# Hybrid encoder layer on one core: the warm-up's tile, the squares of x, the order of SyncE's transfers and the return of the gated heads

## The chip, the cores and the metric

The kernel runs on one core of one Trainium2 chip. The metric is device time in microseconds; the program is run several times and the median counts. All matrix work is in 32-bit floats, split in two parts as told below.

## The reference, cut to what matters

One layer of the encoder is computed: pre-norm, neighbourhood attention over an 8 x 64 grid of tokens, a gate, the projection out, post-norm, residual. With 512 tokens, width 2048, 16 heads of 128:

```
h = x * rsqrt(mean(x*x) + eps) * g_pre
q, k, v, z = split(h @ w_in)            # 2048 x 8192
o = softmax(q k^T * scale + bias) v     # keys: all 8 rows, 16 columns round the query's
y = (o * silu(z)) @ w_out               # 2048 x 2048
out = x + y * rsqrt(mean(y*y) + eps) * g_post
```

## The kernel before, in words

**Split operands.** Each matrix operand is split into `hi` (a cast on ScalarE, ACT, L227) and `lo` (the rest, a subtraction on VectorE, DVE, L228), and a product is three matmuls: hi by hi, hi by lo, lo by hi. The part of x is called `a` (L136, L137), after a scaling by the pre-norm's gain (L140, `gcol`).

**Blocks.** The main loop (L662) walks over blocks m. A block is one k tile of 128 rows: a weight tile of 128 x 512 is brought in (`raw`, four buffers, or `T`, eight tiles), split (three buffers of `hi` and of `lo`), and multiplied with the parts of x. `prep` (L217) of a block runs two blocks ahead of its matmuls, and at its end issues later loads (`load_raw`, `load_t`).

- Blocks 0 to 31 (`mm_first`, L264) are the projection in for heads 0 and 1, twelve matmuls each. In the first sixteen x comes in too (`load_x`, L129, three blocks ahead of its own).
- Then seven steps, one for each further pair of heads, of seven passes of eight blocks with six matmuls each (`mm_in`, L285; accumulators u1X to u7Z by step and chain). This is a product in seven instead of eight parts, so weights are added up on VectorE first (`t<-t,raw`, L224). The fifth and the seventh pass of a step load new T tiles while raws come in.
- Blocks 424 to 487 (`mm_out`, L629) are the projection out, four quarters n of sixteen blocks, twelve matmuls each.

**Beside the blocks.** `at(m, f)` hangs work on a block: for each head the transposes (`turn`, L358), the splits of q and k, the scores (L422, tiles `s`), the bias table (`load_bias`, `bias`, L405: `braw` and `bm`), exponentials and normalization (`edge`, `p`), the second transpose and its split (`pt`), the product with v (L492, `o`), the gate (`gate0` to `gate2`, `gated`, `zm`). While step s is projected, the heads of the pair before are attended to; heads 14 and 15 run in the projection out. The gated heads 0 to 13 are written to memory by GpSimd (`graw`, L504), come back late in step 7 and in the projection out (`gr`, L514, one tile of the tag "z" each), and are split into `g` (L520, L521) for the blocks of the projection out: head k in block k of each quarter.

**Squares.** Sixteen tiles of x in token order (`square_x`, `sq`) are squared and summed on ScalarE (L164) for the pre-norm; `rstd` turns the sums into `rc`, with which the results of the projection are scaled (`take_first`, L271).

**What sets the order.** Each engine runs its instructions in one queue, and SyncE (SP) issues nearly all loads in one queue too: a load that waits for its buffer holds the loads behind it. The code is written in the order of the blocks, but a scheduler sorts each engine's queue when the program is built, by its own estimate of when things are ready. So the written order and the built order differ. Pools matter: the tag "c" has six pair tiles (128 x 2 x 512) that hold the results of a pair's projection, and later `yg`.

**The warm-up.** Eight small matmuls of the identity (`warm`, L86, sixteen records in the trace) are written first, to keep TensorE busy until there is data.

Of the kernel before, what the change touches and what calls it, by code (L numbers as in the profile page):

```python
# [15 lines left out]
P = 128  # L16
# [34 lines left out]

@with_exitstack
def na_block(ctx: ExitStack, tc: tile.TileContext, xT, x, gpre, gpost, w_in, w_out, rpb, mask, out):
    nc = tc.nc
    PSUM = bass.MemoryType.PSUM
# [27 lines left out]
    make_identity(nc, ident)  # L83
    warm = px.tile([P, P], F32, tag="T", name="warm")
    for i in range(WARM):
        nc.tensor.matmul(warm, ident, ident, start=True, stop=True)  # L86
# [26 lines left out]
    def load_t(step, q, k):  # L113
        nc.sync.dma_start(T[k], w_in[step, q, k])
# [4 lines left out]
    def load_x(k):  # L119
        kk = k % KH  # L120
        if k >= KH:
            X[k] = small("v" if kk < 4 else "z", f"x{k}")
        elif kk < 4:
            X[k] = small("qk", f"x{k}")
        else:
            if kk % 2 == 0:
                X["c", kk] = pair(f"x{k}")
            X[k] = X["c", kk - kk % 2][:, kk % 2, :]
        nc.sync.dma_start(X[k], xT[k])  # L129
# [25 lines left out]
    def square_x(i):  # L155
        j, n = divmod(i, 4)
        ns = slice(n * L, (n + 1) * L)
        t = sp.tile([P, L], F32, tag=("bm", "braw")[i % 2], name=f"sq{i}")
        if j == 0:
            nc.sync.dma_start(t[0:64, :], x_v[56:64, :, ns])  # L160
            nc.sync.dma_start(t[64:128, :], x_v[0:8, :, ns])
        else:
            nc.sync.dma_start(t, x_v[16 * j - 8 : 16 * j + 8, :, ns])
        return lambda: nc.scalar.activation(t, t, AF.Square, accum_out=part[:, j, n : n + 1])  # L164
# [31 lines left out]
    def load_raw(m):  # L196
# [10 lines left out]
        nc.sync.dma_start(raws[m], src)  # L207
# [299 lines left out]

    def split_g(h):

        if h in g_of:  # L510
            g = g_of[h]
        else:
            g = small("z", f"gr{h}")
            nc.gpsimd.dma_start(g, graw[h])  # L514

        def go():
            k, o = h % KH, h // KH
            t = ag.tile([P, 2, L], F32R, tag=f"a{k}_{1 - o}", name=f"g{h}")
            hi, lo = t[:, 0, :], t[:, 1, :]
            nc.scalar.copy(hi, g)  # L520
            nc.vector.tensor_tensor(lo, g, hi.bitcast(F32), ALU.subtract)  # L521
            G[h] = (hi, lo)

        return go
# [32 lines left out]
    def when(h, c):  # L557

        pr, b = divmod(h, 2)
        m = base(pr + 1)  # L560
        return m + c + (3, 26)[b] if pr < NSTEP - 1 else m + (1, 8)[b] + c * 3 // 10

    for h in range(HEADS):
        for c, f, *args in HEAD:
            at(when(h, c), f, h, *args)
        last = h == HEADS - 1
        at(when(h, 0) - (2 if last else 11), load_bias, h)
        for i in range(3):
            at(when(h, 0) - (0 if last else 7 - i), bias, h, i)
# [4 lines left out]
    done = {}  # L574

    def fetch_g(h):
        done[h] = split_g(h)

    for h in range(HEADS):
        if h < HEADS - 2:  # L580
            m, wait = (NIN - SLOTS + 30 + 3 * h, 4) if h < KH else (NIN + h - KH, 3)
            at(m, fetch_g, h)
            at(m + wait, lambda h=h: done.pop(h)())
        else:
            at(when(h, 23), lambda h=h: split_g(h)())
# [6 lines left out]
    for i in range(16):  # L592
        at(2 + i, begin, i)
        at(4 + i, lambda i=i: pending.pop(i)())
    at(8, lambda: nc.gpsimd.dma_start(mask_sb, mask))
    at(20, rstd)
    for j in range(4):
        at(22 + j, take_first, 0, j)
# [55 lines left out]
    def load_res(t, q):  # L654
        xres[t, q] = spare(4 * t + q)
        nc.sync.dma_start(xres[t, q], x_v[16 * t : 16 * t + 16, :, q * L : (q + 1) * L])
# [5 lines left out]
    for m in range(-AHEAD, N):  # L662
# [10 lines left out]
        else:  # L673
            n, k = divmod(m - NIN, KT)
            if k == 4:
                gb[n] = T[n]
                nc.sync.dma_start(gb[n], gpost[n * L : (n + 1) * L].partition_broadcast(P))
# [66 lines left out]
```

## Time and profile before

| | us |
|---|---|
| median of 3 runs | 922.99 (922.83 to 924.97) |
| the profiled execution's own time | 921.92 |
| its span, first to last instruction | 920.1 |
| TensorE busy (matmuls) | 892.3 |
| VectorE busy | 691.0 |
| ScalarE busy | 536.9 |
| mean granted clock of TensorE | 0.992 |
| moved by DMA | 171.72 MB |

The profile has TensorE as PE (matmuls) and PEld (weight loads), VectorE as DVE, ScalarE as ACT, GpSimd as POOL and SyncE's queue as SPq. A row of a timeline is: start, duration, engine, line, operation, output<-inputs without buffer numbers, shape, count, and in brackets how long the engine was idle before and what ended it. A row of waits is: total us, times, longest. Line numbers in rows are those of the kernel before.

### The profile page before, as it was taken

The page shows a single profiled execution, that of the slowest core. Times are in us where ns is not written, and L with a number is a line of the kernel's source. Part 1 is how long each engine was busy: PE and PEld are TensorE (multiplying, and loading weights), DVE is VectorE, ACT ScalarE, POOL GpSimd, SP SyncE. Part 2 cuts the span into 40 slices and gives each one's busy share as a digit, 9 for nine tenths or more (in the row PEclk, how much of TensorE's full clock was granted, in tenths as well). Part 3 has the DMA queues.
Part 4 walks back from the last instruction along what each step waited for, and adds up shares of the span by engine and source line. Part 5 has one row for each costly group of instructions (what it writes and reads, how often), then busy time and mean ns, then how long its engine had stood idle before and what let it go on. Part 6 is the DMA issues. An engine that isn't in the chain of part 4 may idle for free.

```text
span 920.1 us, 13073 instructions
## 1 busy us (share of the span) xinstructions
PE 892.3 (97%) x4224; PEld 740.1 (80%) x4224; DVE 691.0 (75%) x1279; ACT 536.9 (58%) x1049; POOL 36.1 (4%) x63
## 2 busy tenths in 40 slices
PE   7989999999999999999999999999989799999995
PEld 6868888888888888888888888888877688888884
DVE  3765679897989889888979897989788665232336
ACT  6764566575758566765675576648575555232322
POOL 0000000000000000000000000000001000000004
PEclk9999999999999999999999999999999899999998
DMA  7884346755684777376747765785678942333335
GB/s 235 266 231 134 95 133 215 242 192 166 225 267 130 213 223 252 113 230 212 241 134 228 222 227 145 229 246 170 184 237 273 277 145 68 104 92 103 93 91 183
DMA packets 91637, 171.72 MB, mean 187 GB/s; under 512 B 10656, under 2 KB 10656, under 8 KB 91568
## 3 DMA queue, kind: packets, MB, share of 16 engines
q1 hardware_dynamic: 87840, 159.95, 56.4%
q0 software_dynamic: 3296, 10.41, 4.3%
q8 instruction: 33, 0.54, 0.2%
q10 hardware_dynamic: 432, 0.53, 0.2%
q14 instruction: 36, 0.29, 0.1%
HBM read 162.98 MB, written 7.86 MB: 186 GB/s over the span
## 4 chain that ended last, share of the span: by engine, by line
PE 65%; issue 21%; DMA 7%; DVE 3%; ACT 1%; POOL 1%; SPq 0%; DVEq 0%; POOLq 0%; ACTq 0%
PE u L264 4%; PE u6Y L285 4%; PE u3Y L285 4%; PE u2Y L285 4%; PE u5Y L285 4%; PE u4Y L285 4%; PE u1Y L285 3%; DMA raw<-in_w_in 3%; PE u5Z L285 2%; PE u3X L285 2%; PE u1X L285 2%; PE u2X L285 2%; PE u6X L285 2%; PE u5X L285 2%; PE u4X L285 2%
## 5 line engine op out<-in xcount | busy, mean ns | idle before, releaser
L228 DVE TENSOR_TENSOR lo<-raw,hi 128x512 fp32r<-128x512 f32 x208 | 142.2, 690 | 159.4 <-ACT hi L227 136.5
L227 ACT CAST hi<-t 128x512 fp32r<-128x512 f32 x280 | 171.0, 618 | 111.7 <-DVE t L224 30.1
L227 ACT CAST hi<-raw 128x512 fp32r<-128x512 f32 x208 | 128.0, 621 | 161.5 <-PE y L629 79.1
L228 DVE TENSOR_TENSOR lo<-t,hi 128x512 fp32r<-128x512 f32 x280 | 189.9, 684 | 12.1 <-ACT hi L227 8.4
L629 PE MATMUL y<-hi,g 128*128 128x512 f32 x512 | 160.5, 394 | 0.0
L224 DVE TENSOR_TENSOR t<-t,raw 128x512 f32<-128x512 f32 x224 | 150.1, 686 | 10.6 <-DMA raw<-in_w_in 9.6
L629 PEld LDWEIGHTS y<-hi,g 128*128 128x128 f32 x512 | 95.8, 189 | 20.7 <-DVE yg L642 0.6
L629 PE MATMUL y<-lo,g 128*128 128x512 f32 x256 | 100.5, 393 | 0.0
L264 PE MATMUL u<-hi,a 128*128 128x512 f32 x256 | 66.7, 399 | 9.1 <-ACT hi L227 9.0
L264 PEld LDWEIGHTS u<-hi,a 128*128 128x128 f32 x256 | 48.6, 191 | 20.7 <-ACT hi L227 10.8
L629 PEld LDWEIGHTS y<-lo,g 128*128 128x128 f32 x256 | 48.5, 189 | 10.0
L264 PE MATMUL u<-lo,a 128*128 128x512 f32 x128 | 35.3, 390 | 0.2 <-DVE lo L228 0.2
L137 DVE TENSOR_TENSOR a<-x,a 128x512 fp32r<-128x512 f32 x32 | 21.7, 687 | 11.7 <-ACT a L136 11.5
L405 DVE TENSOR_TENSOR bm<-braw,mask_sb 128x256 f32<-128x256 f32 x48 | 27.6, 597 | 2.8 <-DMA braw<-in_rpb 2.8
L264 PEld LDWEIGHTS u<-lo,a 128*128 128x128 f32 x128 | 24.0, 188 | 5.7 <-DVE lo L228 0.7
L334 ACT ACTIVATE s<-s,rc 128x512 f32<-128x512 f32 x28 | 20.1, 719 | 12.6 <-DVE s L321 12.0
L285 PE MATMUL u1Y<-hi,a 128*128 128x512 f32 x96 | 26.8, 396 | 0.0
L285 PE MATMUL u4Y<-hi,a 128*128 128x512 f32 x96 | 26.8, 396 | 0.0
L285 PE MATMUL u3Y<-hi,a 128*128 128x512 f32 x96 | 26.8, 396 | 0.0
L285 PE MATMUL u2Y<-hi,a 128*128 128x512 f32 x96 | 26.8, 396 | 0.0
L285 PE MATMUL u6Y<-hi,a 128*128 128x512 f32 x96 | 26.8, 396 | 0.0
L285 PE MATMUL u5Y<-hi,a 128*128 128x512 f32 x96 | 26.8, 396 | 0.0
(399 smaller groups left out, 1793.2 us busy)
## 6 DMA issues: line engine op xcount, KB each, us to landing
raw<-in_w_in SPq DMA_DIRECT2D x368, 256.0 KB, 3.1
t<-in_w_in SPq DMA_DIRECT2D x112, 256.0 KB, 4.2
raw<-in_w_out SPq DMA_DIRECT2D x64, 256.0 KB, 2.7
x<-in_xT SPq DMA_DIRECT2D x16, 256.0 KB, 4.4
spare<-in_x SPq DMA_DIRECT2D x16, 256.0 KB, 7.3
graw<-zm POOLq DMA_DIRECT2D x14, 256.0 KB, 4.2
gr<-graw POOLq DMA_DIRECT2D x14, 256.0 KB, 4.5
out<-spare SPq DMA_DIRECT2D x14, 256.0 KB, 3.1
```

Source lines behind the costliest of these rows:

```text
L137: nc.vector.tensor_tensor(lo, src, hi.bitcast(F32), ALU.subtract)
L224: nc.vector.tensor_tensor(T[k], T[k], src, ALU.add)
L227: nc.scalar.copy(hi, src)
L228: nc.vector.tensor_tensor(lo, src, hi.bitcast(F32), ALU.subtract)
L264: nc.tensor.matmul(U[n][j], l, r, start=k == 0 and i == 0, stop=k == KT - 1 and i == 2)
L285: nc.tensor.matmul(U[c][s], l, r, start=p in (0, 1, 4) and k == 0 and n == 0, stop=k == KH - 1 and n == 2, skip_group_check=True,)
L334: nc.scalar.activation(t[:, s, :], t[:, s, :], AF.Copy, scale=rc[:, j + s : j + s + 1])
L405: nc.vector.tensor_tensor(bm[:, i, :].rearrange("p (a b) -> p a b", b=8), rev, mask_sb[:, i, :].unsqueeze(2).to_broadcast([P, 32, 8]), ALU ...
L629: nc.tensor.matmul(Y[n][t], l[:, tsl], r, start=k == 0 and i == 0, stop=k == KT - 1 and i == 2)
```

## The change

Five edits:

1. The warm-up multiplies a tile `ones`, which VectorE fills with one memset; it borrows the buffer of the tag "bm". Before it multiplied `ident`, which GpSimd makes in two instructions.
2. The squares of x begin at blocks 3 to 25, two in three blocks, instead of 2 to 17, one in each; `rstd` moves from block 20 to 28 and `take_first` of the first half from 22 to 25 to 28 and 29.
3. SyncE's loads go through `InOrder`, which asks the scheduler to keep each in the order in which it is written. The stores of the result still go through the plain engine.
4. The gated heads come back two at a time into a pair tile of the tag "c", from ten blocks before the projection out to seven blocks into it, and are split two blocks before their use (`early`).
5. Head 14 starts one block later; the bias of heads 0 and 15 is loaded four blocks ahead and added beside the head's own first blocks.

```diff
+class InOrder:
+    def __init__(self, tc, engine):
+        self.tc, self.engine = tc, engine
+    def __getattr__(self, name):
+        f = getattr(self.engine, name)
+        return lambda *args, **kwargs: self.tc.keep_in_program_order(f(*args, **kwargs))
...
+    sync = InOrder(tc, nc.sync)
...
+    ones = sp.tile([P, P], F32, tag="bm", name="ones")
+    nc.vector.memset(ones, 1.0)
     warm = px.tile([P, P], F32, tag="T", name="warm")
     for i in range(WARM):
-        nc.tensor.matmul(warm, ident, ident, start=True, stop=True)
+        nc.tensor.matmul(warm, ones, ones, start=True, stop=True)
...
-        nc.sync.dma_start(T[k], w_in[step, q, k])
+        sync.dma_start(T[k], w_in[step, q, k])
...
+    def fetch_g(h):
+        t = pair(f"gr{h}")
+        for i in range(2):
+            nc.gpsimd.dma_start(t[:, i, :], graw[h + i])
+            g_of[h + i] = t[:, i, :]
+
     def split_g(h):
-        if h in g_of:
-            g = g_of[h]
-        else:
-            g = small("z", f"gr{h}")
-            nc.gpsimd.dma_start(g, graw[h])
...
-        return m + c + (3, 26)[b] if pr < NSTEP - 1 else m + (1, 8)[b] + c * 3 // 10
+        return m + c + (3, 26)[b] if pr < NSTEP - 1 else m + (2, 8)[b] + c * 3 // 10
...
-        last = h == HEADS - 1
-        at(when(h, 0) - (2 if last else 11), load_bias, h)
+        late = h in (0, HEADS - 1)
+        at(when(h, 0) - (4 if late else 11), load_bias, h)
         for i in range(3):
-            at(when(h, 0) - (0 if last else 7 - i), bias, h, i)
+            at(when(h, i) if late else when(h, 0) - 7 + i, bias, h, i)
...
+    def early(c):
+        return NIN + c if c >= 0 else NIN + 2 * c
+
     for h in range(HEADS):
         if h < HEADS - 2:
-            m, wait = (NIN - SLOTS + 30 + 3 * h, 4) if h < KH else (NIN + h - KH, 3)
-            at(m, fetch_g, h)
-            at(m + wait, lambda h=h: done.pop(h)())
+            if h % 2 == 0:
+                at(early(h - 5), fetch_g, h)
+            at(early(h - 2), split_g, h)
...
     for i in range(16):
-        at(2 + i, begin, i)
-        at(4 + i, lambda i=i: pending.pop(i)())
+        at(3 + i + i // 2, begin, i)
+        at(5 + i + i // 2, lambda i=i: pending.pop(i)())
     at(8, lambda: nc.gpsimd.dma_start(mask_sb, mask))
-    at(20, rstd)
+    at(28, rstd)
     for j in range(4):
-        at(22 + j, take_first, 0, j)
+        at(28 + j // 2, take_first, 0, j)
```

The other loads of SyncE (x, squares, raw, the post-norm's gain, the residual's x) go from `nc.sync` to `sync` in the same way.

**What stands in the queues, at three places.** The first is the start, on TensorE and ScalarE. TensorE before, from its first row; `u` are accumulators, `hi`, `lo` and `a` as above:

```order
L264 MATMUL u_0_184<-hi_156,a_0_105 128x512
L264 MATMUL u_1_185<-hi_156,a_0_105 128x512
L264 MATMUL u_2_186<-hi_156,a_0_105 128x512
L264 MATMUL u_3_187<-hi_156,a_0_105 128x512
L264 MATMUL u_0_184<-hi_156,a_0_105 128x512
L264 MATMUL u_1_185<-hi_156,a_0_105 128x512
L264 MATMUL u_2_186<-hi_156,a_0_105 128x512
L86 MATMUL warm<-ident 128x128 x8
L264 MATMUL u_3_187<-hi_156,a_0_105 128x512
```

TensorE in the changed program, from its first row:

```order
L100 MATMUL warm<-ones 128x128 x8
L278 MATMUL u_0_186<-hi_158,a_0_107 128x512
L278 MATMUL u_1_187<-hi_158,a_0_107 128x512
L278 MATMUL u_2_188<-hi_158,a_0_107 128x512
L278 MATMUL u_3_189<-hi_158,a_0_107 128x512
```

The warm-up stood behind seven matmuls of block 0 and now stands first. ScalarE at the same place, before; the number behind `x`, `hi`, `raw` and `a` is the block, and the pair tile `x4` holds x of blocks 4 and 5:

```order
L140 ACTIVATE x3_182<-x3_182,gcol_78 128x512
L227 CAST hi3_203<-raw3_160 128x512
L136 CAST a3_0_114<-x3_182 128x2x256
L140 ACTIVATE x4_209<-x4_209,gcol_78 128x512
L136 CAST a4_0_117<-x4_209 128x2x256
L140 ACTIVATE x4_209<-x4_209,gcol_78 128x512
L227 CAST hi4_226<-raw4_162 128x512
```

and in the changed program:

```order
L241 CAST hi3_205<-raw3_162 128x512
L241 CAST hi4_228<-raw4_164 128x512
L154 ACTIVATE x3_184<-x3_184,gcol_78 128x512
L241 CAST hi5_250<-raw5_173 128x512
L150 CAST a3_0_116<-x3_184 128x2x256
L154 ACTIVATE x4_211<-x4_211,gcol_78 128x512
L150 CAST a4_0_119<-x4_211 128x2x256
```

The casts of blocks 4 and 5 moved ahead of the `a` tile of block 3. The second place is SyncE's queue in the first blocks, before (`sq` are the squares' tiles):

```order
L207 DMA raw5_171<-in_w_in 128x512
L129 DMA x3_182<-in_xT 128x512
L207 DMA raw6_180<-in_w_in 128x512
L129 DMA x4_209<-in_xT 128x512 x2
L160 DMA sq0_245<-in_x 64x1x512
L161 DMA sq0_245<-in_x 64x1x512
L207 DMA raw7_207<-in_w_in 128x512
```

and in the changed program:

```order
L60 DMA raw5_173<-in_w_in 128x512
L60 DMA raw6_182<-in_w_in 128x512
L60 DMA x3_184<-in_xT 128x512
L60 DMA raw7_209<-in_w_in 128x512
L60 DMA x4_211<-in_xT 128x512
L60 DMA raw8_232<-in_w_in 128x512
L60 DMA x4_211<-in_xT 128x512
```

Each load of x now stands behind one raw load more, and the squares come later. The third place is VectorE in step 7, where head 13's q is split (`q13l`); `raw402` is the raw tile of block 402, in the fifth pass. Before:

```order
L224 TENSOR_TENSOR t3_132<-t3_132,raw403_7213 128x512
L224 TENSOR_TENSOR t4_133<-t4_133,raw404_7238 128x512
L365 SCALAR_TENSOR_TENSOR q13l_7200<-tq13_7181,q13h_7199 128x512
L228 TENSOR_TENSOR lo399_7210<-t7_136,hi399_7209 128x512
L224 TENSOR_TENSOR t5_134<-t5_134,raw405_7256 128x512
L228 TENSOR_TENSOR lo400_7234<-t0_129,hi400_7233 128x512
```

and in the changed program:

```order
L238 TENSOR_TENSOR t3_134<-t3_134,raw403_7215 128x512
L379 SCALAR_TENSOR_TENSOR q13l_7202<-tq13_7183,q13h_7201 128x512
L242 TENSOR_TENSOR lo399_7212<-t7_138,hi399_7211 128x512
L242 TENSOR_TENSOR lo400_7236<-t0_131,hi400_7235 128x512
L449 ISA edge0_100,mx13_7275<-s13_0_7227,bm13_6982 128x192
```

The additions for blocks 404 and 405 are gone from this place; they stand further back.

More of the change, by code (lines that the diff above doesn't have):

```diff
@@ L128, in load_x @@
             X[k] = X["c", kk - kk % 2][:, kk % 2, :]
-        nc.sync.dma_start(X[k], xT[k])
+        sync.dma_start(X[k], xT[k])
     def split_a(k, src, o):
@@ L159, in square_x @@
         if j == 0:
-            nc.sync.dma_start(t[0:64, :], x_v[56:64, :, ns])
-            nc.sync.dma_start(t[64:128, :], x_v[0:8, :, ns])
+            sync.dma_start(t[0:64, :], x_v[56:64, :, ns])
+            sync.dma_start(t[64:128, :], x_v[0:8, :, ns])
         else:
-            nc.sync.dma_start(t, x_v[16 * j - 8 : 16 * j + 8, :, ns])
+            sync.dma_start(t, x_v[16 * j - 8 : 16 * j + 8, :, ns])
         return lambda: nc.scalar.activation(t, t, AF.Square, accum_out=part[:, j, n : n + 1])
@@ L206, in load_raw @@
             src = w_out[n, k]
-        nc.sync.dma_start(raws[m], src)
+        sync.dma_start(raws[m], src)
     W = {}
@@ L506, in na_block @@
     G = {}
-    def split_g(h):
-        if h in g_of:
-            g = g_of[h]
-        else:
-            g = small("z", f"gr{h}")
[L514 to L524, printed above, removed]
+    def fetch_g(h):
[3 more added lines that the diff above has]
+            g_of[h + i] = t[:, i, :]
+    def split_g(h):
+        k, o = h % KH, h // KH
+        t = ag.tile([P, 2, L], F32R, tag=f"a{k}_{1 - o}", name=f"g{h}")
+        hi, lo = t[:, 0, :], t[:, 1, :]
+        nc.scalar.copy(hi, g_of[h])
+        nc.vector.tensor_tensor(lo, g_of[h], hi.bitcast(F32), ALU.subtract)
+        G[h] = (hi, lo)
     beside = {}
@@ L572, in na_block @@
         at(base(pr + 1) + 2, split_v, pr, 1)
-    done = {}
-    def fetch_g(h):
-        done[h] = split_g(h)
+    def early(c):
+        return NIN + c if c >= 0 else NIN + 2 * c
     for h in range(HEADS):
         if h < HEADS - 2:
-            m, wait = (NIN - SLOTS + 30 + 3 * h, 4) if h < KH else (NIN + h - KH, 3)
-            at(m, fetch_g, h)
-            at(m + wait, lambda h=h: done.pop(h)())
+            if h % 2 == 0:
+                at(early(h - 5), fetch_g, h)
+            at(early(h - 2), split_g, h)
         else:
-            at(when(h, 23), lambda h=h: split_g(h)())
+            at(when(h, 23), split_g, h)
     pending = {}
@@ L655, in load_res @@
         xres[t, q] = spare(4 * t + q)
-        nc.sync.dma_start(xres[t, q], x_v[16 * t : 16 * t + 16, :, q * L : (q + 1) * L])
+        sync.dma_start(xres[t, q], x_v[16 * t : 16 * t + 16, :, q * L : (q + 1) * L])
     for k in range(3):
@@ L676, in na_block @@
                 gb[n] = T[n]
-                nc.sync.dma_start(gb[n], gpost[n * L : (n + 1) * L].partition_broadcast(P))
+                sync.dma_start(gb[n], gpost[n * L : (n + 1) * L].partition_broadcast(P))
             if n == 2 and k % 4 == 3:
```

## The prediction

> **What bounds the kernel now.** I read the page's busy times first, then the windows by stage, then who makes TensorE wait, and then went into the two stretches where it does. Page and windows (length, then busy time of PE, weight loads, DVE, ACT and POOL, granted clock, DMA share, GB/s):
>
> ```profile
> PE 892.3 (97%) x4224; PEld 740.1 (80%) x4224; DVE 691.0 (75%) x1279; ACT 536.9 (58%) x1049; POOL 36.1 (4%) x63
> ```
>
> ```profile
> 0.00:70.00 70.00, 60.66 (x256) 48.92 (x257) 42.42 (x83) 50.84 (x101) 3.42 (x12) 1.00 0.81 242
> 190.00:310.00 120.00, 120.00 (x588) 100.43 (x587) 106.01 (x201) 82.47 (x161) 2.69 (x5) 1.00 0.61 186
> 670.00:740.00 70.00, 61.37 (x280) 49.48 (x279) 54.90 (x108) 41.91 (x87) 7.66 (x14) 0.95 0.89 264
> 740.00:900.00 160.00, 160.00 (x733) 131.92 (x732) 60.54 (x109) 55.95 (x114) 0.50 (x1) 1.00 0.32 92
> 900.00:920.10 20.10, 10.68 (x48) 8.50 (x46) 14.86 (x19) 4.96 (x10) 8.72 (x8) 0.82 0.67 209
> ```
>
> TensorE bounds the kernel: from 190 to 310 it never idles, nor from 740 to 900. A change can gain only where it idles or runs slowly: 9.3 us before 70, 8.6 us between 670 and 740, and the tail. The waits of TensorE (total us, times, longest) name nearly all of it:
>
> ```profile
> PE u L264 <- ACT hi L227: 9.0, 4, 5.7
> PE s L422 <- ACT q14h L364: 3.8, 1, 3.8
> PE s L422 <- DVE q13l L365: 2.1, 1, 2.1
> PE u7Z L285 <- ACT hi L227: 1.2, 2, 1.0
> PE u7Z L285 <- DVE lo L228: 0.9, 2, 0.6
> PE o L492 <- DVE pt_1l L371: 0.5, 1, 0.5
> ```
>
> In the first row 5.7 us are the wait for the first data, which stays; 3.3 us are stalls. The other rows are the late stretch: 8.5 us. The start, in order of time:
>
> ```profile
> 5.74 3.35 PE L264 MATMUL u<-hi,a 128*128 128x512 f32 x7 [5.74 <-ACT hi L227]
> 8.89 3.25 PE L86 MATMUL warm<-ident 128*128 128x128 f32 x16
> ...
> 13.14 2.00 PE L264 MATMUL u<-hi,a 128*128 128x512 f32 x8
> ...
> 15.89 0.39 PE L264 MATMUL u<-hi,a 128*128 128x512 f32 x1
> ```
>
> Seven real matmuls come first, one each 0.45 us; then the warm-up takes 3.0 us; from 13.14 a block of twelve takes 2.75 us, 0.229 each (a block is one k tile of 128 rows with all its products). The warm-up stands behind the work that it should warm, and in its way. Late, after the longest wait, the clock is halved as well:
>
> ```profile
> 715.00:720.00 5.00, 3.84 (x15) 2.71 (x16) 5.00 (x10) 3.61 (x7) 1.10 (x2) 1.00 1.05 282
> ...
> 725.00:730.00 5.00, 1.16 (x6) 0.68 (x5) 2.99 (x5) 2.61 (x5) 0.00 (x0) 0.84 1.06 265
> 730.00:735.00 5.00, 5.00 (x17) 4.27 (x16) 2.37 (x8) 2.82 (x7) 0.17 (x1) 0.50 1.06 259
> ```
>
> At 0.50 the five busy microseconds do the work of 2.5; with the edges about 3.0 us are lost to the clock.
>
> **Part 1, the warm-up.** A memset of one tile replaces one that needed a select behind it, and the built order now has the warm-up first. Before, POOL's memset of this size was short:
>
> ```profile
> 0.74 0.21 POOL masks.py:197 MEMSET ident<- 128x128 f32 x1 [0.29 <-POOLq L737]
> ```
>
> So the warm-up starts at 1.0 to 1.5 and, at its 3.0 to 3.3 us, ends before 5.74: its time leaves the path. How soon the clock is fast is not in this trace. Bounds: slow for at least 3.2 us after TensorE's first work (5.74 to 8.89) and at most 7.4 (to 13.14). Counted from 1.3, fast at 4.5 to 8.7. Blocks 0 to 2 are 36 matmuls: all at 0.229 they end at 14.0; with seven at 0.45 at 15.5. Block 3 cannot follow at once. ScalarE's rows of the same place before:
>
> ```profile
> 11.36 0.72 ACT L140 ACTIVATE x<-x,gcol 128x512 f32<-128x512 f32 x1 [2.19 <-DMA x<-in_xT]
> 12.41 0.62 ACT L227 CAST hi<-raw 128x512 fp32r<-128x512 f32 x1 [0.34 <-PE u L264]
> 12.94 0.62 ACT L136 CAST a<-x 128x512 fp32r<-128x512 f32 x1
> ```
>
> A hi tile waits for the block three earlier (three buffers). The new order of ScalarE has hi of block 5 ahead of the a tile of block 3, so that tile comes two casts after block 2 ends: 2 x 0.62 and two handovers, 1.4 us of new stall. Block 3 then starts between 15.4 and 16.9, against 18.6 before (15.89 and one block more): gain 1.7 to 3.2. I take **2.2**.
>
> The Trainium skill (TensorE: Matmul & The Clock Gate, Part 1: The HAM clock gate) says that the clock is halved until one whole window of about 3.4 us was busy, the windows running free, and is halved again after an idle one; the rows agree with the second (3.8 us idle, then 0.50). By the first, a 3.3 us warm-up with a gap behind it may fill no window, and the term would be that of rival B.
>
> **Part 2, squares later, transfers in written order: the start.** The 3.3 us of stalls are hi casts queued on ScalarE behind squares whose rows had not landed:
>
> ```profile
> ACT sq L164 <- DMA sq<-in_x: 10.1, 9, 2.6
> ```
>
> Two squares in three blocks instead of three take a third of their 4 MB out of the worst stretch, and rstd moves from block 20 to 28, where the casts have three blocks (8 us) before step 1 needs the banks. I count **+3.3**. But the written order has a price on SyncE: x of a block now stands behind the raw tile that waits for the lo split of the block before. Durations, and landing times (last column):
>
> ```profile
> L228 DVE TENSOR_TENSOR lo<-raw,hi 128x512 fp32r<-128x512 f32 x208 | 142.2, 690 | 159.4 <-ACT hi L227 136.5
> ```
>
> ```profile
> raw<-in_w_in SPq DMA_DIRECT2D x368, 256.0 KB, 3.1
> ...
> x<-in_xT SPq DMA_DIRECT2D x16, 256.0 KB, 4.4
> spare<-in_x SPq DMA_DIRECT2D x16, 256.0 KB, 7.3
> ```
>
> From x landed: its scaling 0.7, hi 0.6, lo 0.7, the raw's issue 0.4, then the x two blocks on is issued and lands 3.2 (the lone one at 11.36 above, issued at 8.1) to 4.4 later: 5.6 to 6.8 us for two blocks that TensorE does in 5.5. Over the 12 blocks that is 0.6 to 7.8 us. With fewer squares about I take a landing of 3.5: **-2.0**.
>
> **Part 3, written order in the steps.** In the fifth pass of each step the eight T loads now stand between the raws, each waiting for the lo split of its block, and hold the raw behind it. Sixteen transfers of 262 KB in eight blocks of six matmuls, 1.37 us each. A stretch of before in which T and raw loads went out close together, by its window:
>
> ```profile
> 358.00:366.00 8.00, 8.00 (x37) 6.60 (x36) 7.80 (x13) 4.81 (x9) 0.00 (x0) 1.00 0.98 340
> ```
>
> At 340 GB/s they need 12.3 us in 11.0. A raw is used four blocks (5.5 us) after its place; 0.65 goes to the issues and 1.3 to add and hi, so a landing up to about 3.5 us is hidden, and 3.1 is the median. I take **-1.0** for the seven steps; bounds 0 and 7 x 1.8 = -12.6 (landings of 5.3).
>
> **Part 4, the late stretch.** Why TensorE waited there, on ScalarE and VectorE:
>
> ```profile
> 724.87 0.62 ACT L227 CAST hi<-raw 128x512 fp32r<-128x512 f32 x1 [3.63 <-DMA raw<-in_w_out]
> ...
> 728.65 0.60 ACT L364 ACTIVATE q14h<-tq 128x512 fp32r<-128x512 f32 x1
> ```
>
> ```profile
> 672.63 1.41 DVE L224 TENSOR_TENSOR t<-t,raw 128x512 f32<-128x512 f32 x2 [2.15 <-DMA raw<-in_w_in]
> ```
>
> The 3.8 us and the halved clock: q14h stood behind a cast whose raw landed late, because the built order had the sixteen 256 KB loads of x for the residual (7.3 us to land) between the raws. They go to the third quarter of the projection, where the DMAs are 0.32 busy and raws are four blocks (11 us) ahead: cost nothing. (Were that cover gone, sixteen at 0.77 us each would be 12 us.) What is late next: q14h now has casts of gated heads ahead of it, the last of which (head 12) waits for a load issued only when head 9's split frees the pair. A POOL issue, a landing, two casts:
>
> ```profile
> 664.92 0.56 POOL L514 DMA_DIRECT2D gr<-graw  x1
> ```
>
> ```profile
> gr<-graw POOLq DMA_DIRECT2D x14, 256.0 KB, 4.5
> ```
>
> From head 9's split some 0.6 + 3 to 4.5 + 1.2 us pass; other work of the two engines fills about 4: 0.8 to 2.5 left, I take **-1.3**, too short to halve the clock (3.8 did, 2.1 did not). The 2.1 us: VectorE stood at the addition for block 403, whose raw was in flight with the gr load of 664.92, with q13l behind it. No gr load leaves that early now, since its pair must first be freed by head 13's transposes, and one addition less (block 404's) stands ahead of q13l. But then four gr loads leave POOL in a row, beside raws at their densest: **-1.0** (0 to -2). The Trainium skill (DMA: Bandwidth & Descriptors, Issuing engines are not separate DMA queues) says that loads of all issuers share the 16 DMA engines, so a pair on POOL saves none of that; the 2.15 us wait, with gr in flight, agrees. The 1.2 + 0.9 us: VectorE was full (5.00 of 5.00). Its order has 21 operations in the last pass instead of 26: 21 x 0.6 = 12.6 us against 11.0 of TensorE and two blocks (2.7) of lead: **-0.5** left. Late sum: 8.5 + 3.0 - 1.3 - 1.0 - 0.5 = **+8.7**, bounds 5 and 11.5.
>
> The tail from 900 has the same instructions in the same order: 0.
>
> **Sum.** 2.2 + 3.3 - 2.0 - 1.0 + 8.7 = 11.2. The profiled execution's span of 920.1 becomes 908.9; its time was 921.92, 1.8 more, which gives 910.7. The median of the runs, 922.99, is 1.1 above it: I predict **911.5**.
>
> **Rivals.** (A) *First blocks paced by x*: landings of 4.4 cost 7.8 instead of 2.0, time 917.3; for it the median of 4.4, against it the lighter load. 0.12. (B) *The warm-up warms nothing*: the clock comes up where it did, near 11.9. Then 13.7 matmuls are done at 0.45, the other 22.3 end at 17.0, block 3 starts at 18.4: 0.2 instead of 2.2, time 913.5. 0.18. (C) *Slower*: the raws behind the T loads in the fifth pass. At a landing of 5.6 each step loses 2.1, seven lose 14.7 against the other terms' 12.2, and from there it loses; at 6.0, 7 x 2.5 = 17.5, time 928. For it: 12.3 us of transfers in 11.0; against it: it asks for landings nearly twice the median. 0.06. (D) *The late wait only moves*: q14h waits 3.8 again and the clock halves: 2.5 + 3.0 more, time 917. 0.08. (E) all small terms at their kind ends, 3.2 + 3.3 - 0.6 + 11.5 = 17.4 gained: 905.3. 0.06. (F) A and part of C together, about 921: no change. 0.06. The forecast has 0.44.
>
> **Range.** Within 0.3% (2.8 us, about what a measurement here tells from nothing) of 922.99 lies F; C is slower; all else is faster: 0.88, 0.06, 0.06. From 904 to 919 holds all but C, F and the far part of E.
>
> **What would show it.** Step 1 began before at
>
> ```profile
> 102.64 1.07 PE L285 MATMUL u1X<-hi,a 128*128 128x512 f32 x4
> ```
>
> Right: TensorE's first rows are the warm-up, before 2 us; matmuls at 0.23 before 9 us; block 3 near 16; step 1 starts near 99; no wait of ScalarE on sq over 1 us; no loads of x into the spare tiles before 790; no granted 0.50 between 700 and 740; q14h's wait 0.5 to 2.5 us. Wrong: waits of TensorE on hi or lo in every step between its fourth and sixth pass (C), ScalarE idle before x scaling at blocks 4 to 15 (A), matmuls at 0.45 up to 11 us (B).

## The result, and the profile after

| | before | changed |
|---|---|---|
| median of the runs | 922.91 (921.68 to 924.97, 4 runs) | 935.17 (930.49 to 946.25, 4 runs) |
| ratio, with its 95% interval | | 1.0114 (1.0068 to 1.0159) |
| a second set of runs of the same kernel | 922.24 | 933.38, ratio 1.0117 (1.0071 to 1.0163) |

The change makes the kernel about 1.1% slower; 911.5 was predicted. The profile that came with the first set is of a disturbed execution (946.25 us), which the ratio leaves out; the rows below are of an execution of the second set. Its own time is 939.76, 6.4 above the median of that set, so it shows the losses at their upper end: span 938.0 against 920.1.

The page's busy times, and windows of the changed kernel as those of before were shown (length, busy time of PE, weight loads, DVE, ACT, POOL, granted clock, DMA share, GB/s):

```profile
PE 903.3 (96%) x4224; PEld 734.9 (78%) x4224; DVE 692.7 (74%) x1280; ACT 538.9 (57%) x1049; POOL 35.9 (4%) x63
```

```profile
0.00:70.00 70.00, 65.61 (x268) 51.80 (x269) 43.06 (x83) 47.20 (x91) 1.61 (x10) 1.00 0.67 204
190.00:310.00 120.00, 116.18 (x556) 94.88 (x557) 103.89 (x198) 78.98 (x155) 2.68 (x5) 1.00 0.60 182
310.00:430.00 120.00, 116.95 (x571) 96.23 (x571) 102.51 (x188) 74.47 (x144) 2.71 (x5) 1.00 0.62 192
...
760.00:920.00 160.00, 160.00 (x733) 131.78 (x732) 59.89 (x107) 54.44 (x110) 1.96 (x2) 1.00 0.42 119
```

Look at the second row against before's 120.00 (x588). There TensorE never idled; now it idles 3.8 us of the 120, and 32 matmuls fewer are done, which at 0.229 each are 7.3 us (a few records may be missing from a count). The granted clock is 1.00 there, so it is not the clock that was lost. Idle time alone understates the loss, since it counts from the modelled end of the matmul before, which lies behind the start that the next one would have had: at the longest stall of step 2 two matmuls begin 2.15 us apart instead of 0.23, and the idle time there is 1.76 (worked out from the rows of the matmuls). The count, or the length of a step as below, shows it better.

The waits of TensorE now (total us, times, longest) are spread over all steps:

```profile
PE u L278 <- ACT hi L241: 2.2, 2, 1.3
PE u1Y L299 <- ACT hi L241: 2.0, 1, 2.0
...
PE u2Y L299 <- ACT hi L241: 1.8, 1, 1.8
PE u4Y L299 <- ACT hi L241: 1.6, 1, 1.6
PE u4Z L299 <- DVE lo L242: 1.6, 2, 1.2
PE u3Y L299 <- ACT hi L241: 1.5, 1, 1.5
...
PE s L436 <- ACT q14h L378: 1.0, 1, 1.0
```

The late wait for q14h is down from 3.8 to 1.0 as predicted; waits on hi and lo in the chains Y and Z of every step have come instead. They are worth more than their sum of idle time. Where each step's time went, by pass (from the first matmul of a pass to that of the next, mean over steps 2 to 6, worked out from the rows of the matmuls of the chains X, Y and Z):

| pass | 1 | 2 | 3 | 4 | 5 | 6 | 7 | step |
|---|---|---|---|---|---|---|---|---|
| before | 13.0 | 11.6 | 13.3 | 13.8 | 10.9 | 13.3 | 10.9 | 86.9 |
| changed | 13.2 | 11.6 | 13.3 | 13.8 | 11.6 | 14.8 | 13.1 | 91.3 |

A step is 4.4 us longer: 0.7 in the fifth pass, 1.4 in the sixth, 2.2 in the seventh. Here is the cause, in SyncE's queue. Before, around the fifth pass of step 2:

```profile
232.07 7.19 SPq L207 DMA_DIRECT2D raw<-in_w_in  x6
239.54 8.97 SPq L114 DMA_DIRECT2D t<-in_w_in  x6
248.60 0.86 SPq L207 DMA_DIRECT2D raw<-in_w_in  x2
250.43 0.93 SPq L114 DMA_DIRECT2D t<-in_w_in  x2
252.14 10.07 SPq L207 DMA_DIRECT2D raw<-in_w_in  x8
```

and in the changed kernel, whose step 2 begins 3.3 us later:

```profile
226.72 7.93 SPq L60 DMA_DIRECT2D raw<-in_w_in  x8
242.46 0.33 SPq L60 DMA_DIRECT2D t<-in_w_in  x1
242.84 0.42 SPq L60 DMA_DIRECT2D raw<-in_w_in  x1
244.41 0.33 SPq L60 DMA_DIRECT2D t<-in_w_in  x1
244.78 0.43 SPq L60 DMA_DIRECT2D raw<-in_w_in  x1
...
255.99 0.33 SPq L60 DMA_DIRECT2D t<-in_w_in  x1
256.36 10.59 SPq L60 DMA_DIRECT2D raw<-in_w_in  x8
```

Before, six raws went out from 232.07 on, since VectorE's additions free raw buffers well ahead of the matmuls, and the T loads followed. Now the queue issues nothing from 234.65 to 242.46: the first T load waits for the lo split of its block, and the raw behind it waits along. Counted from the start of step 2 (190.4 before, 193.7 now, worked out from the matmuls), that raw goes out at 49.2 us instead of 41.7. The head start of 7.5 us is gone, and each further raw goes out behind its T. TensorE feels it a little in the fifth pass and more in the sixth, here of step 2. POOL, ScalarE, then TensorE:

```profile
256.75 0.53 POOL L413 DMA_DIRECT2D braw<-in_rpb  x1 [22.82 <-DVE bm L419]
```

```profile
262.84 0.62 ACT L241 CAST hi<-raw 128x512 fp32r<-128x512 f32 x1 [3.52 <-DMA raw<-in_w_in]
```

```profile
263.51 1.19 PE L299 MATMUL u2Y<-hi,a 128*128 128x512 f32 x4 [1.76 <-ACT hi L241]
```

The raw issued at 256.36 shares the DMAs with a bias table issued 0.4 us later and with the T load of 255.99; ScalarE gets it at 262.84, some 6.5 us after its issue. The same raw of steps 1 to 4 took 6.3 to 6.7 us, and TensorE idled 1.5 to 2.0 for it; in steps 5 and 6 it took 5.6 and 4.6, and TensorE idled 0.2 and not at all (worked out from the rows of the queue, of ScalarE and of TensorE).

### The profile page after: what moved, and what is told of

Same layout as the page of the kernel before. It is cut to its first block, busy times and chain, and to the rows that moved or that the text cites. A ratio compares the mean times of both kernels' runs of the same rounds, so it can differ in the third digit from the quotient of the medians.

```text
span 944.4 us, 12931 instructions
## 1 busy us (share of the span) xinstructions
PE 907.4 (96%) x4224; PEld 738.3 (78%) x4224; DVE 692.7 (73%) x1280; ACT 538.7 (57%) x1049; POOL 35.9 (4%) x63
## 4 chain that ended last, share of the span: by engine, by line
PE 48%; issue 21%; DMA 13%; DVE 11%; ACT 5%; POOL 1%; SPq 1%; DVEq 0%; ACTq 0%; POOLq 0%
DMA raw<-in_w_in 9%; DVE lo L242 5%; PE u L278 4%; PE u6Y L299 3%; PE u1Y L299 3%; ACT hi L241 3%; PE u7Y L299 3%; PE u2Y L299 2%; PE u4Y L299 2%; PE u1X L299 2%; PE u4X L299 2%; PE u5X L299 2%; PE u6X L299 2%; PE u2X L299 2%; PE u7X L299 2%
## 5 line engine op out<-in xcount | busy, mean ns | idle before, releaser
L299 PE MATMUL u7Y<-hi,a 128*128 128x512 f32 x96 | 27.6, 405 | 0.4 <-ACT hi L241 0.4
```

The source lines that it names most:

```text
L299: nc.tensor.matmul(U[c][s], l, r, start=p in (0, 1, 4) and k == 0 and n == 0, stop=k == KH - 1 and n == 2, skip_group_check=True,)
```

## The experiments

Times are medians in us beside the kernel before on the same chip; a ratio is to the kernel before, with its 95% interval. The stage lengths of the profiled executions (step 1 begins at its first matmul; step 7 ends with the first matmul of the projection out, which is counted to its last; the tail of some 10 us is left out):

| kernel | median | ratio (interval) | step 1 begins | steps 1 to 6 | step 7 | projection out |
|---|---|---|---|---|---|---|
| before | 922.9 | | 102.6 | 522.0 | 93.3 | 192.4 |
| e0, changed | 933.38 | 1.0117 (1.0071, 1.0163) | 101.6 | 548.5 | 90.4 | 187.6 |
| e1, plain queue | 923.54 | 1.0013 (0.9990, 1.0036) | 99.0 | 522.7 | 89.3 | 200.4 |
| e2, order alone | 939.91 | 1.0171 (1.0136, 1.0205) | 101.2 | 544.3 | 95.3 | 185.6 |
| e4, T later | 919.40 | 0.9966 (0.9946, 0.9985) | 98.0 | 531.5 | 93.0 | 186.2 |
| e5, weights free | 913.72 | 0.9909 (0.9887, 0.9930) | 101.3 | 525.9 | 88.3 | 188.0 |
| e6, T on GpSimd | 918.43 | 0.9952 (0.9928, 0.9977) | 99.6 | 528.0 | 89.7 | 188.0 |
| e7, warm-up alone | 919.46 | 0.9964 (0.9946, 0.9983) | 98.3 | 524.4 | 92.3 | 192.7 |
| e8, squares alone | 925.24 | 1.0023 (1.0004, 1.0041) | 105.7 | 522.8 | 92.9 | 190.7 |
| e9, best | 909.88 | 0.9853 (0.9825, 0.9881) | 98.7 | 523.3 | 88.1 | 187.8 |
| e10, edits 4 and 5 alone | 926.70 | 1.0038 (1.0020, 1.0056) | 103.1 | 524.5 | 88.9 | 201.3 |
| e11, residual's order alone | 916.27 | 0.9917 (0.9892, 0.9941) | 102.9 | 523.0 | 92.2 | 185.7 |
| e12, e5 without edit 2 | 913.04 | 0.9890 (0.9865, 0.9915) | 99.4 | 523.9 | 89.1 | 188.1 |
| e13, e9 with longer warm-up | 912.73 | 0.9868 (0.9837, 0.9899) | 97.2 | 524.3 | 88.0 | 190.3 |
| e14, T of fifth pass later | 930.37 | 1.0082 (1.0056, 1.0108) | 97.0 | 541.2 | 92.4 | 186.2 |
| e15, T of seventh pass later | 933.05 | 1.0089 (1.0062, 1.0117) | 98.2 | 540.0 | 93.5 | 187.7 |

### Is it the written order, and by what means?

**e0**, the changed kernel again.

> The changed kernel once more, for a profile of an ordinary run of it. Before, steps 2 to 6 of the projection in take 86.8 us each; in the first profile of the changed kernel they take 90.6 to 93.2. Theory (written order: in a step's fifth and seventh pass each raw load stands behind a T load, which waits for the lo split of its own block): again every step is longer than 86.8, by 2 to 6 us, with TensorE waiting on hi or lo in the fifth to seventh pass; time 930 to 937. Rival (the long steps belong to that one execution): steps of 86.8 to 88 in this profile.

Steps 1 to 7 took 90.4 to 92.1 us each in this profile, and the median is 933.38 us: the long steps are no accident of one execution.

**e1**, the changed kernel without edit 3:

```diff
-    sync = InOrder(tc, nc.sync)
+    sync = nc.sync
```

> The changed kernel with SyncE's loads in the order the scheduler chooses, the other four edits kept. Theory (the written order costs the steps): steps 2 to 6 return to 86.8 us, and the time is that of before less what the warm-up, the squares and the late stretch bring: 914 to 922. Rival 1 (another edit, such as the pair tiles taken by the gated heads or the squares, makes the steps longer): steps stay at 89 to 93 us, time 930 to 937. The residual's x should come early again, so some of the late wait for q14h may be back (up to 3.8 us and 3 us of halved clock).

**e2**, the kernel before with edit 3 alone (the class, and all of SyncE's loads through it):

```diff
+    sync = InOrder(tc, nc.sync)
...
-        nc.sync.dma_start(T[k], w_in[step, q, k])
+        sync.dma_start(T[k], w_in[step, q, k])
...
-        nc.sync.dma_start(raws[m], src)
+        sync.dma_start(raws[m], src)
...
```

> The kernel before with edit 3 alone: SyncE's loads in written order, all else as before. Theory: steps of 89 to 93 us, 7 x 2 to 6 us more, against which only the late stretch gains up to 7 us since the residual's x comes later: 930 to 945. Rival 1 (another edit costs the time): steps of 86.8 us, time 916 to 923.

Without the order, steps 1 to 6 fall back to 522.7 us; with the order alone they take 544.3. The theory's steps are as expected in both. That e1 ends at 923.54 and not at 914 to 922 was a miss: its projection out is 8 us longer than before, of which more below. e2's waits of TensorE show the same rows as the changed kernel:

```profile
PE u3Y L297 <- ACT hi L239: 1.5, 1, 1.5
PE u4Z L297 <- ACT hi L239: 1.3, 2, 0.9
...
PE u5Z L297 <- ACT hi L239: 1.2, 2, 0.9
```

The order could cost by holding raws behind waiting T loads, or because T and raw transfers together are too many. **e4** keeps the written order and every byte, and writes the T loads at later blocks, where their tiles have long been free:

```diff
-            if p == 4:
-                load_t(step, B12, k)
-            elif p == 6 and step + 1 < NSTEP:
-                load_t(step + 1, B11, k)
+            for q, wait in ((4, 8), (6, 4)):
+                if m - wait >= FIRST and where(m - wait)[1] == q:
+                    s, _, kk = where(m - wait)
+                    if q == 4:
+                        load_t(s, B12, kk)
+                    elif s + 1 < NSTEP:
+                        load_t(s + 1, B11, kk)
```

> The changed kernel, still with all of SyncE's loads in written order, but the T loads of the fifth pass are written eight blocks later and those of the seventh pass four blocks later, so that no raw load of the fifth pass stands behind a T load that has to wait. The bytes and the number of transfers are the same. Theory (head-of-line waiting in SyncE's queue): steps 2 to 6 at 86.8 to 88 us, time 912 to 920. Rival 2 (T and raw transfers together are too much for the DMAs in those passes, whatever the order): steps of 89 us and more remain, time 928 or more.

**e6** issues the T loads where they were written, on another queue:

```diff
-        sync.dma_start(T[k], w_in[step, q, k])
+        nc.gpsimd.dma_start(T[k], w_in[step, q, k])
```

> The changed kernel with the T loads issued by GpSimd, all of SyncE's other loads in written order: T waits where it waited, but nothing of SyncE's stands behind it, while gated heads, bias tables and T now share GpSimd's queue. Theory (head-of-line waiting): raws run ahead again, steps 2 to 6 at 86.8 to 88.5 us, time 905 to 916. Rival 2 (too many transfers together, whatever the queue): steps of 89 us or more, time 925 or more.

Both take most of the loss away: steps 1 to 6 at 531.5 and 528.0 us instead of 548.5, 919.40 and 918.43 us in all (e6 a little above what was expected, e4 with steps of up to 90.1). The raw that stands behind the first T load of the fifth pass tells why. Its issue, in us from the first matmul of its step (steps 1 to 7, worked out from the rows of SyncE's queue and of the matmuls):

| kernel | issue of that raw |
|---|---|
| before | 41.5 to 42.4 |
| changed (e0) | 49.2 to 49.8 |
| e2, order alone | 49.2 |
| e4, T later | 41.5 to 43.3 |
| e6, T on GpSimd | 41.5 to 42.8 |

In every step the written order holds it back by some 7 us, and both ways out let it go again, e6 with all raws in written order and T waiting where it waited. That is head-of-line waiting (a load that waits holds the loads behind it), and not the number of transfers: e6's first T load of step 2 goes out at 50.0 us after the step's start, e0's at 48.8. Whether some contention stays is not shown: e6 has steps of up to 88.8 us against 86.8, but e12, with all weights in the scheduler's order, has one of 88.7 as well.

**e14** and **e15** undo the one and the other of e4's two moves: the waits in the new lines are (4, 8), (6, 0) in e14 and (4, 0), (6, 4) in e15.

> The changed kernel, all in written order, with the T loads of the fifth pass alone written eight blocks later; those of the seventh pass as in the changed kernel. With both later the steps took 87.4 to 90.1 us, with none 90.5 to 92. Theory (both passes lose, the fifth more: its raws come late for the sixth, where the stall of about 2 us and a slow spell stand): steps 2 to 6 at 88 to 90 us, time 920 to 926. Rival (the loss is the fifth pass's alone, as the prediction's rival had it): steps as with both later, 918 to 921.

> The changed kernel, all in written order, with the T loads of the seventh pass alone written four blocks later. Theory: the stalls of the fifth and sixth pass stay, those of the seventh go: steps 2 to 6 at 89 to 91 us, time 925 to 931. Rival (the loss is the fifth pass's alone): steps of 90.5 to 92 as in the changed kernel, time 931 to 937.

Their passes, worked out as above:

| pass | 1 | 2 | 3 | 4 | 5 | 6 | 7 |
|---|---|---|---|---|---|---|---|
| e14, fifth's T later | 13.0 | 11.6 | 13.3 | 13.9 | 10.9 | 13.3 | 13.8 |
| e15, seventh's T later | 15.0 | 11.6 | 13.3 | 13.9 | 11.4 | 14.3 | 11.0 |

Each edit cures its own passes and not the others (e14's seventh is even longer than e0's 13.1). The T loads of the fifth pass cost the fifth and sixth (2.1 us a step in the changed kernel), those of the seventh the seventh (2.2). e15 gained next to nothing all the same, since it loses 2 us in the first pass of the next step (15.0 instead of 13.0), where TensorE waits for `lo`:

```profile
PE u2X L302 <- DVE lo L242: 1.8, 2, 1.3
PE u5X L302 <- DVE lo L242: 1.7, 2, 1.3
```

VectorE's row at the start of step 3 (277.31) tells what held `lo` up:

```profile
278.46 0.69 DVE L238 TENSOR_TENSOR t<-t,raw 128x512 f32<-128x512 f32 x1 [2.03 <-DMA raw<-in_w_in]
```

In all six steps of e15 that begin behind another, VectorE stands 1.3 to 2.0 us at an addition whose raw has not landed, with the `lo` splits of the first pass and the combining of the step before queued behind it. No wait in this profile names a load of T. In e4, with both moves, the first pass doesn't suffer (13.0): the raws go out at the same place (2.7 us before the step's start, e15's 2.7 to 3.2), but the built order of VectorE has the other work ahead of the addition, which comes 3.0 us into each step and finds its raw landed. So e15 measures one thing more than its T loads, a new order on VectorE.

Both expectations of time were too kind (930.37 and 933.05 measured). By its time alone e15 would lie with its rival (931 to 937); its fifth to seventh passes are what speaks against the rival.

### The late stretch

**e5** gives the weights back to the scheduler's order and leaves the other loads in written order:

```diff
-        sync.dma_start(T[k], w_in[step, q, k])
+        nc.sync.dma_start(T[k], w_in[step, q, k])
...
-        sync.dma_start(raws[m], src)
+        nc.sync.dma_start(raws[m], src)
```

> The changed kernel with the weight loads (raw and T) back in the order that the scheduler chooses, and the loads of x, of the squares, of the post-norm's gain and of the residual's x still in written order. Theory (only the weights' written order costs, the residual's brings): step 1 begins at 98 to 102 us, steps 2 to 6 take 86.8 us as with the plain queue, step 7 about 89, the projection out 186 as in the two runs with written order: 98 + 88 + 5 x 86.8 + 89.5 + 186 + 10 is a span of 905.5, time 905 to 911. Rival (the residual's order is not what shortens the projection out): 917 or more, with a wait for q14h of 4 us or more.

913.72 us, 19.7 less than the changed kernel, with the late stretch kept: step 7 and the projection out take 276.3 us together, 9.3 less than before. It missed its 905 to 911. The profiled execution (915.45) began step 1 at 101.3, late in the expected range, and lost 4 us in step 3, where one lo came 2.3 us late and the clock halved behind it.

**e10**, edits 4 and 5 alone on the kernel before (the diff of the change's `fetch_g`, `split_g`, `early`, `when` and the bias), and **e11**, written order on the kernel before for two kinds of load:

```diff
-                nc.sync.dma_start(gb[n], gpost[n * L : (n + 1) * L].partition_broadcast(P))
+                sync.dma_start(gb[n], gpost[n * L : (n + 1) * L].partition_broadcast(P))
...
-        nc.sync.dma_start(xres[t, q], x_v[16 * t : 16 * t + 16, :, q * L : (q + 1) * L])
+        sync.dma_start(xres[t, q], x_v[16 * t : 16 * t + 16, :, q * L : (q + 1) * L])
```

> The kernel before with edits 4 and 5 alone, SyncE's queue as the scheduler orders it, so that the residual's x comes early. Theory (the late gain needs the residual's loads out of the way): step 7 falls from 93.3 to about 89 us, but q14h waits 5 to 10 us in the projection out, which grows from 192.4 to 195 to 200: time 921 to 926. Rival (the pair tiles and the later head are what shortens the late stretch): 914 to 918.

> The kernel before with written order for the loads of the post-norm's gain and the residual's x alone. Theory (these loads cause the wait for q14h and the halved clock): the projection out falls from 192.4 to 186 to 188 us, step 7 stays near 93: time 916 to 919. Rival (edits 4 and 5 are needed too): projection out 190 or more, 920 to 924.

e11 alone brings 0.83% (0.59 to 1.08), 6 to 7 us of it in the projection out. e10 alone loses: 926.70, a little above what was expected. Its wait, and ScalarE's rows ahead of it:

```profile
PE s L434 <- ACT q14h L376: 10.1, 1, 10.1
```

```profile
734.29 0.62 ACT L532 CAST g<-gr 128x512 fp32r<-128x512 f32 x1 [4.73 <-DMA gr<-graw]
737.09 0.62 ACT L532 CAST g<-gr 128x512 fp32r<-128x512 f32 x1 [2.18 <-DMA gr<-graw]
...
738.61 0.60 ACT L376 ACTIVATE q14h<-tq 128x512 fp32r<-128x512 f32 x1
```

q14h now stands behind casts of gated heads that come back late, the more so as the residual's sixteen loads are in flight. With those loads moved to the third quarter the same queue costs 1.0 us or less (e0, e5, e9), 1.6 in e13. So edits 4 and 5 shorten step 7 by 4.4 us (93.3 to 88.9) and need the residual's order not to lose it twice over. This is what e1 ran into: its q14h waited 9.6 us.

### The start

**e7**, edit 1 alone on the kernel before, and **e8**, edit 2 alone:

```diff
+    ones = sp.tile([P, P], F32, tag="bm", name="ones")
+    nc.vector.memset(ones, 1.0)
...
-        nc.tensor.matmul(warm, ident, ident, start=True, stop=True)
+        nc.tensor.matmul(warm, ones, ones, start=True, stop=True)
```

> The kernel before with edit 1 alone, the warm-up on a tile filled at once. In the changed kernel's two profiles block 0 ran at 0.43 us a matmul up to 10.6 us, in two of the experiments at 0.23 from 5.8 us on, after the same warm-up from 1.06 to 4.42 us and an idle us. Theory (the clock's windows run free of the program, so whether the warm-up fills one is chance): step 1 begins between 99.5 (fast from the start) and 102 us (fast from 10.6), time 919.5 to 923 by run. Rival (the warm-up never helps): 922 to 924 in all runs.

```diff
-        at(2 + i, begin, i)
-        at(4 + i, lambda i=i: pending.pop(i)())
+        at(3 + i + i // 2, begin, i)
+        at(5 + i + i // 2, lambda i=i: pending.pop(i)())
...
-    at(20, rstd)
+    at(28, rstd)
...
-        at(22 + j, take_first, 0, j)
+        at(28 + j // 2, take_first, 0, j)
```

> The kernel before with edit 2 alone, the squares two in three blocks and rstd at block 28, in the scheduler's order. Before, 3.3 us of TensorE's stalls between 50 and 68 us. Theory: 2 to 3.3 us of them go, step 1 begins at 99.3 to 100.6, time 919.5 to 921. Rival (the stalls only move to other blocks, as 36 to 54 us and 95 us in the changed kernel): step 1 at 102 or later, no change.

e7 is faster by 0.36% (0.17 to 0.54), in a profile that had the clock up at once; e8 is slower by 0.23% (0.04 to 0.41), as its rival had it and a little worse. Its squares arrive no earlier, and ScalarE waits for them at other blocks, with hi casts behind:

```profile
72.07 0.63 ACT L164 ACTIVATE sq<-sq 128x512 f32<-128x512 f32 x1 [5.53 <-DMA sq<-in_x]
...
74.97 1.26 ACT L271 ACTIVATE c<-u,rc 128x512 f32<-128x512 f32 x2 [1.66 <-POOL rc L169]
76.12 0.61 ACT L227 CAST hi<-raw 128x512 fp32r<-128x512 f32 x1
```

**e9** is what these point to, the changed kernel without edit 2 and with written order for the gain and the residual's x alone; **e12** is e5 without edit 2, so that x stays in written order; both with these lines back:

```diff
-        at(3 + i + i // 2, begin, i)
-        at(5 + i + i // 2, lambda i=i: pending.pop(i)())
+        at(2 + i, begin, i)
+        at(4 + i, lambda i=i: pending.pop(i)())
...
-    at(28, rstd)
+    at(20, rstd)
...
-        at(28 + j // 2, take_first, 0, j)
+        at(22 + j, take_first, 0, j)
```

> What the runs so far point to: the changed kernel without edit 2 (squares, rstd and take_first as before) and with the written order for the loads of the post-norm's gain and the residual's x alone. Theory (the gain lies in the warm-up and in the late stretch, the squares bring nothing, the weights must not be in written order): step 1 at 98 to 102 us by the clock's luck, 522 us for steps 1 to 6, 88.5 for step 7, 187.5 for the projection out and 10 for the tail: spans of 906 to 910, time 907 to 912. Rival (the squares' edit or the order of the loads of x carries a part of the gain): 914 or more.

> The changed kernel without edit 2 and with the weight loads in the scheduler's order; against the run with free weights (913.7 us) only the squares, rstd and take_first are as before. Theory (edit 2 brings nothing, its stalls only move): 911 to 915. Rival (edit 2 brings the 3.3 us that the prediction gave it): 916 to 918.

e12 stands where e5 stands (913.04 and 913.72): edit 2 brings nothing in this company either. e9 is the fastest of all, 909.88 us, 1.47% (1.19 to 1.75) below the kernel before. Whether the 3 us between e12 and e9 are the order of x and of the squares' loads is unclear, as their intervals overlap. e9's windows at the two places where the kernel before lost most:

```profile
0.00:70.00 70.00, 66.35 (x277) 53.66 (x278) 43.39 (x84) 50.30 (x100) 3.42 (x12) 1.00 0.87 251
...
670.00:740.00 70.00, 68.13 (x323) 55.11 (x322) 58.51 (x114) 45.20 (x93) 7.30 (x14) 1.00 0.64 206
```

They had x256 and x280 before: 21 and 43 matmuls more in 70 us each. (The second window is not quite the same work, as e9 begins the projection out 7.8 us earlier.)

**e13**, e9 with `WARM = 13` instead of 8:

> The version without edit 2 and with written order for the residual's x and the gain alone (909.88 us), with the warm-up 13 instead of 8 matmuls long: it ends near 6.5 us instead of 4.42 and leaves no gap before block 0, which can start at 5.7. So far, with a gap of an idle us, block 0 ran at 0.23 us a matmul at once in some executions and at 0.43 up to 8.9 to 10.6 us in others. Theory (the idle us lets the clock's next window go unfilled, by chance of the window's place): without the gap matmuls run at 0.23 by 8 us at the latest in this profile, step 1 begins at 97.5 to 99, time 907 to 910. Rival (the length of the warm-up doesn't matter): 0.43 us beyond 8.5 us again, and the longer warm-up costs 0.8 us: 910 to 912.

Its block 0 ran at full speed from 5.84, and step 1 began at 97.2, a little better than the theory's 97.5 to 99; its time (912.73) is not below e9's. In the profiled execution q14h waited 1.6 us and the clock halved behind it. For the time the run is inconclusive.

## Why the prediction was wrong, point by point

**The failed step is Part 3**, "A raw is used four blocks (5.5 us) after its place ... so a landing up to about 3.5 us is hidden, and 3.1 is the median. I take -1.0 for the seven steps". Between e0 and e5, which differ in the order of the weights alone, it measured 933.38 - 913.72 = 19.7 us, 2.8 a step by the medians. (In e0's profile steps 2 to 6 are 4.4 longer than before, but that execution took 6.4 us more than its median.) The mechanism was the one named, that of rival C: raws behind waiting T loads. The term was mis-sized, by two things and against a third.

- *The landing was taken from the wrong place.* 3.1 us is the median of the raws over the whole kernel. The raws that matter travel with T and, in the sixth pass, with a bias table: 6.5 us in the rows above. The prediction's own row of a dense stretch (0.98 of the DMAs) warned of it. A raw used to have a head start over its use; the change took it.
- *One of two places was counted.* The code loads T in the fifth and in the seventh pass; the prediction priced the fifth alone. e14 and e15 split the loss: 2.1 and 2.2 us a step. Rival C, with "at 6.0, 7 x 2.5 = 17.5, time 928", was nearly the result and had 0.06.
- *What is hidden was put too low.* With 3.5 us hidden, a landing of 6.3 to 6.7 would cost 2.8 to 3.2 us. In steps 1 to 4 TensorE lost 1.7 to 2.2 at that raw (the distance of the starts less 0.23), so some 4.5 were hidden there. That error and the missing seventh pass work against each other, and that C's number came so near is in part luck.

**Part 1, the warm-up (+2.2): right in size, partly by luck.** e7 gains 3.3 us (1.6 to 5.0, its ratio on 922.6), which is a mean of two kinds of execution that the sum did not tell apart: near rival B in some, better than the forecast in others. In e0 block 0 ran slowly to 10.7, in e7 fast from the start, after nearly the same warm-up; e0, then e7:

```profile
1.06 3.78 PE L100 MATMUL warm<-ones 128*128 128x128 f32 x16 [1.06 <-DVE ones L97]
5.74 3.78 PE L278 MATMUL u<-hi,a 128*128 128x512 f32 x8 [0.90 <-ACT hi L241]
9.32 1.71 PE L278 MATMUL u<-lo,a 128*128 128x512 f32 x4
10.87 2.00 PE L278 MATMUL u<-hi,a 128*128 128x512 f32 x8
```

```profile
1.06 3.52 PE L88 MATMUL warm<-ones 128*128 128x128 f32 x16 [1.06 <-DVE ones L85]
5.79 2.14 PE L266 MATMUL u<-hi,a 128*128 128x512 f32 x8 [1.21 <-ACT hi L229]
```

Eight matmuls take 3.78 us in the one and 2.14 in the other. Of eleven profiles with this warm-up five were fast at once.

**Part 2, squares later (+3.3) and loads of x in written order (-2.0): the gain failed, the price did not show.** The stalls were laid to squares that wait for their rows, which was so, but spreading them out moved the stalls instead of removing them: ScalarE's wait for sq was 19.7 us in e0 against 10.1:

```profile
ACT sq L178 <- DMA sq<-in_x: 19.7, 11, 3.9
```

That "the casts have three blocks (8 us) before step 1 needs the banks" was wrong as well. In e0 the four `take_first` stand ahead of a hi cast, and TensorE waits 1.26 us at 96.00:

```profile
93.02 2.42 ACT L285 ACTIVATE c<-u,rc 128x512 f32<-128x512 f32 x4 [1.66 <-POOL rc L183]
95.31 1.15 ACT L241 CAST hi<-raw 128x512 fp32r<-128x512 f32 x2
```

Step 1 began at 101.6 in e0 where 99 was forecast. The slow clock of block 0 has its part in that: 4.9 us at the slow clock from 5.74 on, of which about half is lost (an estimate). That the rest is edit 2's missing gain fits e8, where step 1 began at 105.7 instead of 102.6, and e5, which came out 2.9 above 923 - 12.2 = 910.8, the prediction's sum without Part 3; it is not shown. As for the price: in e2, with the order and the old warm-up, step 1 began at 101.2, earlier than the 102.6 of before, and ScalarE's waits for x came to 4.9 us against 4.2, in one profile each. (The prediction's own durations give 5.9 us for two blocks at a landing of 3.5, and thus -2.4 and not -2.0.)

**Part 4, the late stretch (+8.7): right.** 9.3 us in e5. The residual's loads were the cause of the 3.8 us and the 3.0 of halved clock, whose sum of 6.8 stands beside 6.7 in e11's projection out, and the wait of q14h behind "casts of gated heads", put at -1.3, is there at 1.0 us in e0. That it would be 10 us without the residual's order (e10), the sum did not ask. "Too short to halve the clock" held in e0 and not in e13, where a wait of 1.6 us halved it.

**Rivals.** C came true. A, the first blocks paced by x, is not borne out by e2's start. B's sign came in e0 (0.43 us a matmul up to 10.7) and not in e7, and its price of 2.0 is not what made the kernel slower. D is e1's and e10's fate, not the changed kernel's. Of what would show it wrong, the line for C ("waits of TensorE on hi or lo in every step") is the one that decides. The written sum itself gives 922.99 - 11.2 = 911.8, where 911.5 stands; nothing hangs on that.

## What to carry to other kernels

An order fixed by hand in a queue that stops at its first waiting load costs what the loads behind it could have gained by going early: before fixing it, look for the loads that wait on compute (here T on a lo split) and write them where their buffers are already free, or give them another queue. Price a load's landing by the rows of the stretch where it will fly, not by the median of its kind, and list every place where the code issues it. An edit that bundles a gain (the residual's order, 7.7 us by e11's ratio) with a loss of the same mechanism (the weights' order, 19.7) is worth splitting by kind of load.

## What the runs showed of the hardware

The clock's change did not take a window that is wholly busy or wholly idle. Clock changes in a trace lie on a grid of 3.413 us whose place differs from run to run. (The column of the granted clock, the third from the end, reads 1.00 before a trace's first clock record too; at the start the matmuls show the clock, 0.43 us apart or 0.23.) Windows of that grid, e4 at its start, e0 at its start, then e5 and e0 in step 3:

```profile
2.13:5.54 3.41, 2.71 (x13) 2.42 (x12) 0.30 (x1) 2.01 (x4) 0.11 (x1) 1.00 0.97 338
```

```profile
0.43:3.84 3.41, 2.78 (x13) 2.79 (x14) 0.17 (x1) 1.32 (x2) 1.42 (x7) 1.00 0.55 177
...
351.99:355.40 3.41, 1.93 (x10) 1.31 (x9) 0.26 (x1) 0.91 (x2) 0.00 (x0) 1.00 0.70 250
355.40:358.81 3.41, 3.41 (x18) 2.79 (x18) 3.41 (x6) 2.47 (x6) 0.00 (x0) 1.00 0.39 106
```

```profile
353.97:357.38 3.41, 1.43 (x7) 0.85 (x5) 2.85 (x5) 0.93 (x2) 0.55 (x1) 1.00 0.95 294
357.38:360.79 3.41, 3.12 (x7) 2.48 (x8) 3.41 (x7) 2.63 (x6) 0.00 (x0) 0.50 0.81 281
```

The matmuls after the first window (e4) were fast from 5.54 on, with 2.71 of 3.41 us busy; after the second (e0), with 2.78, they stayed slow, so the bound lies about there, as far as modelled ends of matmuls tell. Within the kernel, 1.43 us busy halved the clock for one window (e5) and 1.93 did not (e0). Over all these profiles, windows with up to 1.64 us busy were each followed by the half clock and none from 1.81 up; in between both were seen (worked out from the rows of the matmuls, between the start and the tail). A stall of about 2 us can thus cost a slow window behind it or not, by where it falls: e13's 1.6 us for q14h did, e0's 2.0 us in step 1 did not. The Trainium skill (TensorE: Matmul & The Clock Gate, Part 1: The HAM clock gate) has the clock halved after an idle window; here a window that was over a third busy was enough, and the measurement decides. It also says that the windows run free of the kernel, with which e0 and e7 agree. The prediction's "3.8 did, 2.1 did not" was too simple.
